# Seven Strassen column pairs, each interleaved with an ordinary one, and all their sums on VectorE

## Chip, cores and metric

The kernel runs on one core of one Trainium2 chip. The metric is the device time of one execution in microseconds (us). Three runs of the kernel before took 884.0 us in the median (883.87 to 885.13). Engines are called by the profile's short names: PE (matrix products), PEld (its weight loads), DVE (VectorE), ACT (ScalarE), POOL (GpSimd) and SP, whose queue issues the DMAs.

## The reference

One layer for 512 tokens of width 1024: an mLSTM and an S5 mixer, and behind them a gated feed-forward net with a hidden width of 2816. The change lies in the feed-forward net alone, in its first product:

```python
def _conv_glu_ffn(h, w_ffn_up, w_ffn_conv, b_ffn_conv, w_ffn_down):
    val, gate = jnp.split(h @ w_ffn_up, 2, axis=-1)
    gate = jax.nn.gelu(_causal_dwconv(gate, w_ffn_conv, b_ffn_conv))
    return (gate * val) @ w_ffn_down
...
        h = _standardize(x) * (1.0 + sc2) + sh2
        f = _conv_glu_ffn(h, w_ffn_up[l], w_ffn_conv[l], b_ffn_conv[l], w_ffn_down[l])
        x = _layer_norm(ALPHA * x + (1.0 + g2) * f, ln2_gain[l], ln2_bias[l])
```

`_causal_dwconv` has three taps here. Everything is computed in float32.

## The kernel before

The hidden width is cut into 22 tiles of 128 (`j` = 0 to 21). For each `j` the kernel makes a gate tile and a value tile, each 128 x 512 (channels by tokens), with the 1024 inputs in eight pieces of 128 (`k`). A float32 factor is written as the sum of two fp32r numbers, `hi` and `lo`, and a product is three matmuls: hi·hi, hi·lo, lo·hi (`mm3`, lines 247 to 249). So an ordinary tile is 24 matmuls of 128 x 512, and an ordinary `j` is 48.

The splitting costs ACT and DVE work: ACT casts a weight tile to its high part (line 226), DVE subtracts to get the low part (line 215). `wsplit` does it for an ordinary tile (128 x 1024), from the buffers `w` (two) to `wh` and `wl` (three each).

Ten of the 22 `j` are made by Strassen's scheme in Winograd's form (`fast_pairs`). The gate and value weights of one `j` and the two halves of `k` give a 2 x 2 block matrix, the halves of `k` and of the tokens another. Seven half-size products, each 12 matmuls of 128 x 256 (`prod`, line 1264), stand for eight. Their weight operands are `a11`, `a12`, `a22` and four sums `r3`, `r2`, `r1`, `r4` (`fast_operands`); their `h` operands are quarters of `h2` and four combinations in the `hp` buffers, which `x_combos` makes once. Each weight operand is split by `half` (ACT on line 1227, DVE on line 215). Two sums of products, `d` and the upper half of `cv`, are made on DVE from PSUM, and the second must be read before the next product goes on in the same bank.

In `fast_pairs` two neighbouring `j` go through four parts together: `first` (a, c), `second` (b, a), `third` (b, d), `fourth` (b). The pairs begin at `FAST` = 5, 8, 11, 14, 17, and one ordinary `j` stands between two pairs. Both `a` and both `c` come from the four PSUM banks called `hd`. The same four banks hold the scratch of the gelu (`gate_half`, which calls `gelu2`, lines 566 to 570): ACT squares into the bank, DVE, ACT (tanh) and DVE follow, and the last DVE instruction, `hh<-hd,hh` on line 207, gives the bank back. The names `gtile` (called `acc` in the trace) and `vtile` (`s` in the trace, tag `s5`) are two banks each for gate and value products.

All eight small sums `gtt(...)` of `fast_operands` of a pair, and 16 of the 32 sums of `x_combos`, run on POOL (line 350, which is the helper `gtt`). `MODS` says after which `j` one slice of the last modulation vector (`g2`) is added up: each step is two DMAs of 128 x 512 into `hh` buffers and two DVE instructions into `s5h`. `NSP` = 19: the activations of `j` below 19 are written to DRAM (`spill`) and read again for the down product; those of 19 to 21 stay in SBUF. There are seven `hh` buffers.

The order of each engine's instructions is fixed when the program is built: a scheduler places each engine's work by its own reckoning of when inputs are there. Each engine then works strictly through its row and waits at an instruction until its inputs have come.

Of the kernel before, what the change touches and what calls it, by code (L numbers as in the profile page):

```python
# [162 lines left out]
def _build(ctx, tc, nc, h):  # L163
# [1103 lines left out]
    def fast_operands(j):  # L1267
# [7 lines left out]
        return a11, r3, r2, a12, r1, a22, r4

    def fast_pairs(js):
        src = [fast_operands(j) for j in js]
        a, c, b, d, cv = {}, {}, {}, {}, {}
        for j in js:  # L1280
            b[j], d[j] = gtile[j % 2], vtile[j % 2]

        def op(i, n):
            return half(src[i][n])

        def first(i, j):
            a[j], c[j] = bank("hd"), bank("hd")
            cv[j] = hh()
            prod(a[j], op(i, 0), xq(0, 0), True)
            A.copy(b[j][:, 0:256], a[j][:, 0:256])  # L1290
            prod(c[j], op(i, 1), xc(3), True)
            A.copy(cv[j][:, 0:256], c[j][:, 0:256])

        def second(i, j):
            prod(b[j], op(i, 2), xc(2))
            tt(d[j][:, 0:256], b[j][:, 0:256], cv[j][:, 0:256], ALU.add)
            prod(a[j], op(i, 3), xq(1, 0))

        def third(i, j):
            prod(b[j], op(i, 4), xc(1))  # L1300
            tt(cv[j][:, 256:512], b[j][:, 0:256], cv[j][:, 0:256], ALU.add)
            prod(d[j], op(i, 5), xc(4))

        def fourth(i, j):
            prod(b[j], op(i, 6), xq(1, 1))
# [88 lines left out]
```

## Time and profile before

| | |
|---|---|
| median of 3 runs | 884.0 us |
| the profiled execution: its time / its span | 885.54 / 883.8 us |
| PE busy | 826.0 us (93%), 4466 matmuls |
| DVE busy | 675.0 us (76%), 1240 instructions |
| ACT busy | 391.8 us (44%) |
| POOL busy | 173.7 us (20%) |
| mean granted PE clock | 0.987 of full speed |

The profiled execution took 1.54 us more than the median of the runs. Of its own time 1.7 us lie outside the span, which runs from the first to the last instruction. The first product of the feed-forward net fills the span from about 476 to 753 us, the down product from there to 876 us. In the timeline a row may merge several equal instructions; a start and a duration are given, and in brackets the engine's idle time before it and what ended it. Busy times of DVE overlap a little: an instruction may start before the record of the last one ends.

### The profile page before, as it was taken

Reading aid. Unit: us, or ns where it says so; the run is one execution under the profiler, and the core shown is the slowest. Engines: PE = TensorE matmul, PEld = TensorE weight load, DVE = VectorE, ACT = ScalarE, POOL = GpSimd, SP = SyncE. Lnnn points to the kernel's source line nnn. Section 1 sums busy time; section 2 is a strip of 40 time slices with the busy share of each in tenths; the row PEclk is TensorE's granted clock in tenths of the full one; section 3 lists DMA queues with packets and bytes.
Section 4 is the critical chain, followed back from the end, with each engine's and each line's share of the span. In section 5 each row is a group of like instructions: output and inputs, shape, how many; then the busy total and the mean of one; then the engine's idle time right before and its main releaser. Section 6 shows DMA issues by size and latency. Waiting matters only on the chain.

```text
span 883.8 us, 12383 instructions
## 1 busy us (share of the span) xinstructions
PE 826.0 (93%) x4466; PEld 682.2 (77%) x4466; DVE 675.0 (76%) x1240; ACT 391.8 (44%) x665; POOL 173.7 (20%) x289
## 2 busy tenths in 40 slices
PE   3999999999999999999999889989789998999996
PEld 1777878787777788888888868978778886788885
DVE  5557988789689755579888898797978767999144
ACT  4454565546456432323344555544454444545000
POOL 2771221122121000000003662342222000000000
PEclk9999999999999999999999989999999999999998
DMA  9832121322212445487552055423443243667011
GB/s 342 295 100 83 59 94 57 80 59 67 82 37 89 126 130 180 141 286 239 186 193 75 1 202 167 130 98 110 141 131 120 84 153 121 212 216 239 25 47 48
DMA packets 50893, 115.98 MB, mean 131 GB/s; under 512 B 13968, under 2 KB 14864, under 8 KB 50832
## 3 DMA queue, kind: packets, MB, share of 16 engines
q1 hardware_dynamic: 50832, 115.19, 39.6%
q8 instruction: 35, 0.57, 0.3%
q14 instruction: 26, 0.21, 0.1%
HBM read 105.99 MB, written 7.08 MB: 128 GB/s over the span
## 4 chain that ended last, share of the span: by engine, by line
PE 64%; DVE 21%; ACT 6%; issue 4%; DMA 3%; SPq 2%; POOL 1%; DVEq 0%; ACTq 0%; POOLq 0%
PE acc L247 8%; PE acc L249 8%; PE acc L248 8%; PE hd L247 6%; DVE hh L207 6%; PE hd L248 6%; PE hd L249 6%; PE acc L1264 4%; PE hd L1264 3%; PE s L247 2%; PE s L248 2%; PE s L249 2%; PE s L1264 2%; SPq L197 2%; DVE wl L215 1%
## 5 line engine op out<-in xcount | busy, mean ns | idle before, releaser
L226 ACT CAST wh<-w 128x1024 fp32r<-128x1024 f32 (+2 forms) x83 | 82.4, 995 | 109.7 <-PE acc L248 64.8
L215 DVE TENSOR_TENSOR wl<-w,wh 128x1024 fp32r<-128x1024 f32 (+2 forms) x83 | 99.0, 1195 | 21.9 <-ACT wh L226 19.1
L247 PE MATMUL acc<-hp,wh 128*128 128x512 f32 x256 | 103.3, 404 | 0.4 <-ACT hx L790 0.4
L248 PE MATMUL acc<-hp,wh 128*128 128x512 f32 x256 | 101.9, 398 | 0.0
L249 PE MATMUL acc<-hp,wl 128*128 128x512 f32 x256 | 101.8, 398 | 0.0
L1029 POOL TENSOR_SCALAR mov<-mov 128x1 f32<-128x1 f32 x6 | 4.1, 688 | 344.5 <-ACT acc L1028 172.6
L247 PEld LDWEIGHTS acc<-hp,wh 128*128 128x128 f32 x256 | 48.2, 189 | 14.7 <-issue 3.7
L249 PEld LDWEIGHTS acc<-hp,wl 128*128 128x128 f32 x256 | 48.2, 188 | 11.2 <-issue 0.4
L248 PEld LDWEIGHTS acc<-hp,wh 128*128 128x128 f32 x256 | 48.2, 188 | 10.8 <-issue 0.4
L207 DVE SCALAR_TENSOR_TENSOR s5h<-hh,k,s5h 128x512 f32<-128x512 f32 x56 | 44.9, 842 | 5.9 <-DMA hh<-in_wa 5.9
L207 DVE SCALAR_TENSOR_TENSOR hh<-hd,hh 128x512 f32<-128x512 f32 (+3 forms) x40 | 24.4, 609 | 21.0 <-ACT hd L569 12.3
L350 POOL TENSOR_TENSOR hx<-gab,gab 128x512 f32<-128x512 f32 x10 | 15.1, 1508 | 99.6 <-DMA gab<-in_wup 90.1
L350 POOL TENSOR_TENSOR hx<-gab,hx 128x512 f32<-128x512 f32 x20 | 32.6, 1632 | 4.8 <-DVE hb L215 3.4
L248 PE MATMUL hd<-s5b,wh 128*128 128x512 f32 (+1 forms) x88 | 32.2, 367 | 0.5 <-DVE s5b L215 0.5
L247 PE MATMUL hd<-s5b,wh 128*128 128x512 f32 (+1 forms) x88 | 31.8, 367 | 0.7 <-ACT s5b L1180 0.5
L249 PE MATMUL hd<-s5b,wl 128*128 128x512 f32 (+1 forms) x88 | 31.9, 363 | 0.0
L567 ACT ACTIVATE hd<-hh 128x512 f32<-128x512 f32 x22 | 13.2, 601 | 40.9 <-DVE hh L207 40.8
L248 PE MATMUL acc<-hx,wh 128*128 128x512 f32 x74 | 29.2, 394 | 0.0
L247 PE MATMUL acc<-hx,wh 128*128 128x512 f32 x74 | 29.1, 394 | 0.0
L249 PE MATMUL acc<-hx,wl 128*128 128x512 f32 x74 | 29.1, 393 | 0.0
L1264 PE MATMUL hd<-hp,hb 128*128 128x256 f32 x120 | 17.7, 300 | 11.5 <-DVE hh L207 11.5
L212 DVE TENSOR_TENSOR hh<-w,hh 128x512 f32<-128x512 f32 x42 | 27.3, 685 | 1.1 <-DMA w<-in_wfd 1.1
(626 smaller groups left out, 2392.9 us busy)
## 6 DMA issues: line engine op xcount, KB each, us to landing
hh<-in_wa SPq DMA_DIRECT2D x64, 256.0 KB, 4.2
w<-in_win SPq DMA_DIRECT2D x30, 512.0 KB, 3.3
w<-in_wup SPq DMA_DIRECT2D x24, 512.0 KB, 3.8
w<-in_wfd SPq DMA_DIRECT2D x22, 512.0 KB, 4.1
gab<-in_wup SPq DMA_DIRECT2D x20, 512.0 KB, 3.6
hb<-in_wa SPq DMA_DIRECT2D x16, 512.0 KB, 7.3
spill<-hh SPq DMA_DIRECT2D x19, 256.0 KB, 2.0
hh<-spill SPq DMA_DIRECT2D x19, 256.0 KB, 3.4
```

Of the source, the lines that this page charges most:

```text
L197: return nc.sync.dma_start(o, i)
L207: V.scalar_tensor_tensor(o, i0, s, i1, op0=op0, op1=op1)
L212: V.tensor_tensor(o, a, b, op=op)
L215: V.tensor_tensor(o, a, b, op=ALU.subtract)
L226: A.copy(hi, x)
L247: T.matmul(o, lhsT=wh, rhs=xh, start=first, stop=False)
L248: T.matmul(o, lhsT=wh, rhs=xl, start=False, stop=False)
L249: T.matmul(o, lhsT=wl, rhs=xh, start=False, stop=last)
L350: GP.tensor_tensor(o, a, b, op=op)
L567: A.activation(a, x, AF.Square, scale=GELU_S)
L1029: GP.tensor_scalar(v[:, 2:3], v[:, 0:1], v[:, 1:2], EPS * D, op0=ALU.add, op1=ALU.add)
L1264: T.matmul(o[:, 0:256], lhsT=w[:, p, sl], rhs=x[k][y], start=first and k + i == 0, stop=k == 3 and i == 2, skip_group_check=True)
```

## The change

`fast_pairs` goes. In its place `fast_and_plain(j)` makes `j` by the seven products and `j + 1` in the ordinary way, with the ordinary one's two tiles in halves of 12 matmuls (`part`) between the seven products. `FAST` is now 6, 8, 10, 12, 14, 16, 18, so seven `j` are made by Strassen's scheme, not ten, and 13 by ordinary products behind the two of the start, not ten. The sums of `fast_operands` and of `x_combos` are all on DVE (`tt`), none on POOL. `x_combos` is called before `j` = 3, not 4. `MODS` is 5, 6, 8, 10, 12, 14, 16, 18. `NSP` is 20: the activation of `j` = 19 goes through DRAM too. All split operands now lie in the six `hb` buffers.

```diff
-FAST = (5, 8, 11, 14, 17)
-XJ = 4
-MODS = (7, 10, 10, 13, 13, 16, 16, 19)
-NSP = 19
+FAST = (6, 8, 10, 12, 14, 16, 18)
+XJ = 3
+MODS = (5, 6, 8, 10, 12, 14, 16, 18)
+NSP = 20
...
-    optag = iter((("hb",) * 6 + ("wh", "wl") * 3 + ("hb",) * 2) * NF)
+    optag = iter(("hb",) * (8 * NF))
...
-            gtt(xk[k][:, lo_], f32(h2[k][0])[:, lo_], f32(h2[k][1])[:, lo_], ALU.add)
+            tt(xk[k][:, lo_], f32(h2[k][0])[:, lo_], f32(h2[k][1])[:, lo_], ALU.add)
...
-        gtt(r3, a11, a21, ALU.subtract)
...
+        tt(r3, a11, a21, ALU.subtract)
...
-    def fast_pairs(js):
...
-        for part in (first, second, third, fourth):
-            for i, j in enumerate(js):
-                part(i, j)
-        for j in js:
-            gg = gate_half(j, (a[j], b[j]))
-            val_half(j, gg, (d[j], cv[j][:, 256:512]))
+    def fast_and_plain(j):
+        src = fast_operands(j)
+        b, d = gtile[j % 2], vtile[j % 2]
+        g2_, v2_ = gtile[1 - j % 2], vtile[1 - j % 2]
+        a, c = bank("hd"), bank("hd")
+        cv = hh()
...
+        prod(a, half(src[0]), xq(0, 0), True)
+        A.copy(b[:, 0:256], a[:, 0:256])
+        prod(c, half(src[1]), xc(3), True)
+        A.copy(cv[:, 0:256], c[:, 0:256])
+        wg_ = wsplit(h["wup"][2 * j + 3])
+        part(g2_, wg_, 0)
+        prod(b, half(src[2]), xc(2))
+        tt(d[:, 0:256], b[:, 0:256], cv[:, 0:256], ALU.add)
+        prod(a, half(src[3]), xq(1, 0))
+        part(g2_, wg_, 1)
+        prod(b, half(src[4]), xc(1))
+        tt(cv[:, 256:512], b[:, 0:256], cv[:, 0:256], ALU.add)
+        prod(d, half(src[5]), xc(4))
+        gg2 = gate_half(j + 1, (g2_,))
+        wv_ = wsplit(h["wup"][2 * j + 2])
+        part(v2_, wv_, 0)
+        prod(b, half(src[6]), xq(1, 1))
+        gg = gate_half(j, (a, b))
+        val_half(j, gg, (d, cv[:, 256:512]))
+        part(v2_, wv_, 1)
+        val_half(j + 1, gg2, (v2_,))
```

On PE, the start of the second pair (`j` = 8 and 9) before, one row for each run of matmuls with the same operands; `hd_5843` and `hd_5878` are the two `a`, `hd_5844` and `hd_5879` the two `c`:

```order
L1264 MATMUL hd_5843<-s5b_4721,hb_5846 128x256 x3
L1264 MATMUL hd_5843<-s5b_4722,hb_5846 128x256 x3
L1264 MATMUL hd_5843<-s5b_4723,hb_5846 128x256 x3
L1264 MATMUL hd_5843<-s5b_4724,hb_5846 128x256 x3
L1264 MATMUL hd_5844<-hp_5343,hb_5862 128x256 x6
L1264 MATMUL hd_5844<-hp_5344,hb_5862 128x256 x6
L1264 MATMUL hd_5878<-s5b_4721,hb_5881 128x256 x3
L1264 MATMUL hd_5878<-s5b_4722,hb_5881 128x256 x3
L1264 MATMUL hd_5878<-s5b_4723,hb_5881 128x256 x3
L1264 MATMUL hd_5878<-s5b_4724,hb_5881 128x256 x3
L1264 MATMUL hd_5879<-hp_5343,hb_5897 128x256 x6
L1264 MATMUL hd_5879<-hp_5344,hb_5897 128x256 x6
```

The same place in the changed kernel, at `j` = 10 with the ordinary 11 (`acc_4896` is the gate tile of 11, `hd_5987` and `hd_5988` are `a` and `c` of 10):

```order
L249 MATMUL acc_4896<-s5b_4721,wl_6025 128x512
L247 MATMUL acc_4896<-s5b_4722,wh_6024 128x512
L1264 MATMUL hd_5987<-s5b_4721,hb_5990 128x256 x3
L1264 MATMUL hd_5987<-s5b_4722,hb_5990 128x256 x3
L1264 MATMUL hd_5987<-s5b_4723,hb_5990 128x256 x3
L1264 MATMUL hd_5987<-s5b_4724,hb_5990 128x256 x3
L1264 MATMUL hd_5988<-hp_5271,hb_6006 128x256 x6
L1264 MATMUL hd_5988<-hp_5272,hb_6006 128x256 x6
L248 MATMUL acc_4896<-s5b_4722,wh_6024 128x512
L249 MATMUL acc_4896<-s5b_4722,wl_6025 128x512
```

Before, a pair opens all four `hd` banks at once, 48 matmuls in a row. Now a stage opens two, and matmuls of the ordinary tile stand ahead of them and behind.

On DVE, the rows before the same pair: the gelu of the ordinary `j` = 7 (`hd_5774` is its scratch bank), its value product, and what follows; `hb_6037` and `hb_6052` are low parts of the last operands of the pair 8 and 9, `hb_6210` is the first of the next:

```order
L207 SCALAR_TENSOR_TENSOR hh_5769<-acc_4896,k_63,hh_5769 128x510
L215 TENSOR_TENSOR wh_6006<-hx_5837,wh_6006 128x512
L207 SCALAR_TENSOR_TENSOR hh_5769<-acc_4896,k_63,hh_5769 128x511
L215 TENSOR_TENSOR wl_6022<-gab_5833,wl_6022 128x512
L207 SCALAR_TENSOR_TENSOR hd_5774<-hd_5774,hh_5769 128x512
L207 SCALAR_TENSOR_TENSOR hh_5773<-hd_5774,hh_5769 128x512
L212 TENSOR_TENSOR hh_5773<-s_1059_4898,hh_5773 128x512
L215 TENSOR_TENSOR hb_6037<-hx_5826,hb_6037 128x512
L215 TENSOR_TENSOR hb_6052<-hx_5838,hb_6052 128x512
L201 TENSOR_SCALAR s5h_5811<-hh_5813,k_92 128x512
```

On DVE in the changed kernel, from the sum `d` of `j` = 8 on; `hb_6006` to `hb_6056` are low parts for `j` = 10, `hx_6199` and `hx_6200` sums for `j` = 12, `wl_6127` is the low part of an ordinary tile of 11, `hh_5771` the `cv` of 8, `hh_5896` the gate of 9:

```order
L212 TENSOR_TENSOR s_1058_4897<-acc_4895,hh_5771 128x256
L207 SCALAR_TENSOR_TENSOR s5h_5532<-hh_5754,k_92,s5h_5532 128x512
L215 TENSOR_TENSOR hb_6006<-hx_5979,hb_6006 128x512
L212 TENSOR_TENSOR hx_6199<-hx_6198,gab_6193 128x512
L215 TENSOR_TENSOR hb_6040<-hx_5980,hb_6040 128x512
L212 TENSOR_TENSOR hx_6200<-gab_6193,hx_6198 128x512
L215 TENSOR_TENSOR wl_6127<-w_6124,wh_6126 128x1024
L212 TENSOR_TENSOR hh_5771<-acc_4895,hh_5771 128x256
L207 SCALAR_TENSOR_TENSOR hh_5896<-acc_4896,k_63,hh_5896 128x510
L215 TENSOR_TENSOR hb_6056<-gab_5975,hb_6056 128x512
```

The sums, which stood on POOL, now stand between the splits; the splits on DVE are for the stage after the one that PE is in, the sums for the one after that.

On DVE, the rows before the first ordinary weight of the product (`wl_5198`, for `j` = 2), in the kernel before; `hp_...` are the low parts of the combinations of `h`, `gab_...` holds the combinations themselves:

```order
L212 TENSOR_TENSOR gab_5065<-gab_5065 128x256
L215 TENSOR_TENSOR hp_5344<-gab_5039,hp_5344 128x512
L215 TENSOR_TENSOR hp_5341<-gab_5052,hp_5341 128x512
L215 TENSOR_TENSOR hp_5342<-gab_5065,hp_5342 128x512
L215 TENSOR_TENSOR hp_5339<-gab_5026,hp_5339 128x512
L215 TENSOR_TENSOR hp_5340<-gab_5039,hp_5340 128x512
L215 TENSOR_TENSOR hp_5345<-gab_5052,hp_5345 128x512
L215 TENSOR_TENSOR hp_5346<-gab_5065,hp_5346 128x512
L215 TENSOR_TENSOR wl_5198<-w_5195,wh_5197 128x1024
```

And in the changed kernel:

```order
L212 TENSOR_TENSOR gab_5052<-gab_5052,gab_5026 128x256 x2
L212 TENSOR_TENSOR gab_5052<-gab_5052 128x256 x2
L212 TENSOR_TENSOR gab_5065<-gab_5065,gab_5039 128x256 x2
L212 TENSOR_TENSOR gab_5065<-gab_5065 128x256 x2
L215 TENSOR_TENSOR hp_5271<-gab_5026,hp_5271 128x512
L215 TENSOR_TENSOR hp_5272<-gab_5039,hp_5272 128x512
L215 TENSOR_TENSOR hp_5269<-gab_5052,hp_5269 128x512
L207 SCALAR_TENSOR_TENSOR hh_5171<-hd_4905,k_63,hh_5171 128x510
L215 TENSOR_TENSOR wl_5198<-w_5195,wh_5197 128x1024
```

Sixteen more sums stand ahead of the weight, five of the eight splits have gone behind it, and one instruction of the first gate has come in front of it.

## Rows read from the trace of the kernel before

**Rows 1.** The page: busy time of each engine with its share of the span, and the share of each engine in the chain of waits that ended last.

```profile
PE 826.0 (93%) x4466; PEld 682.2 (77%) x4466; DVE 675.0 (76%) x1240; ACT 391.8 (44%) x665; POOL 173.7 (20%) x289
...
PE 64%; DVE 21%; ACT 6%; issue 4%; DMA 3%; SPq 2%; POOL 1%; DVEq 0%; ACTq 0%; POOLq 0%
```

**Rows 2.** Stretches of the five Strassen pairs, from their first matmul to the next ordinary one: bounds and length in us, busy us (and instructions) of PE, PEld, DVE, ACT and POOL, granted PE clock, DMA share, GB/s.

```profile
547.35:567.05 19.70, 19.70 (x169) 19.70 (x168) 14.55 (x20) 11.10 (x21) 9.23 (x6) 1.00 0.38 121
578.45:604.54 26.09, 21.88 (x170) 21.47 (x169) 21.86 (x29) 13.27 (x25) 6.83 (x5) 0.93 0.37 123
615.93:643.68 27.75, 21.99 (x170) 21.35 (x169) 23.93 (x31) 13.39 (x25) 7.53 (x5) 0.94 0.41 135
655.05:681.98 26.93, 21.90 (x169) 21.48 (x168) 22.59 (x31) 12.85 (x24) 7.83 (x5) 0.94 0.41 138
693.36:713.94 20.58, 20.14 (x170) 19.93 (x169) 13.79 (x21) 9.31 (x16) 0.00 (x0) 1.00 0.42 131
```

**Rows 3.** The same view for two of the four ordinary `j` between the pairs (7 and 16).

```profile
567.05:578.45 11.40, 11.40 (x51) 8.96 (x50) 9.96 (x12) 4.69 (x10) 5.65 (x4) 1.00 0.32 111
...
681.98:693.36 11.38, 11.38 (x50) 8.95 (x49) 9.13 (x16) 6.37 (x12) 0.00 (x0) 1.00 0.06 23
```

**Rows 4.** What PE waited for between 547 and 730 us: total us, times, longest.

```profile
PE hd L1264 <- DVE hh L207: 12.5, 6, 3.8
PE acc L1264 <- DVE s L212: 3.0, 2, 1.5
```

**Rows 5.** PE's timeline: two undisturbed products of the first pair, and the start of the second pair with the wait in it.

```profile
561.39 1.58 PE L1264 MATMUL acc<-hp,wh 128*128 128x256 f32 x12
562.80 1.57 PE L1264 MATMUL s<-hp,wl 128*128 128x256 f32 x12
...
587.34 1.99 PE L1264 MATMUL hd<-hp,hb 128*128 128x256 f32 x12 [3.80 <-DVE hh L207]
589.12 2.76 PE L1264 MATMUL acc<-hp,hb 128*128 128x256 f32 x12
```

**Rows 6.** DVE's timeline ahead of that wait.

```profile
574.67 1.78 DVE L215 TENSOR_TENSOR wh<-hx,wh 128x512 fp32r<-128x512 f32 x1
576.37 1.78 DVE L207 SCALAR_TENSOR_TENSOR hh<-hh,k,hh 128x511 f32<-128x511 f32 x1
...
583.18 0.68 DVE L215 TENSOR_TENSOR wh<-hx,wh 128x512 fp32r<-128x512 f32 x1
583.78 0.74 DVE L207 SCALAR_TENSOR_TENSOR hh<-acc,k,hh 128x511 f32<-128x511 f32 x1
```

**Rows 7.** POOL's timeline in the same stretch.

```profile
575.98 1.63 POOL L350 TENSOR_TENSOR hx<-hx,gab 128x512 f32<-128x512 f32 x1
```

**Rows 8.** Groups of DVE instructions by line and shape between 682 and 753 us, where POOL does nothing: busy us, mean ns of one, and the idle time before them with what ended it.

```profile
L215 DVE TENSOR_TENSOR wl<-w,wh 128x1024 fp32r<-128x1024 f32 x6 | 7.3, 1224 | 2.4 <-ACT wh L226 1.3 <-PE s L1264 1.0
L207 DVE SCALAR_TENSOR_TENSOR hh<-hd,hh 128x512 f32<-128x512 f32 x10 | 6.9, 691 | 4.6 <-ACT hd L569 4.5
L207 DVE SCALAR_TENSOR_TENSOR hd<-hd,hh 128x512 f32<-128x512 f32 x8 | 5.6, 698 | 3.2 <-ACT hd L567 2.9
L207 DVE SCALAR_TENSOR_TENSOR s5h<-hh,k,s5h 128x512 f32<-128x512 f32 x6 | 4.3, 746 | 2.3 <-DMA hh<-in_wa 2.3
L207 DVE SCALAR_TENSOR_TENSOR hh<-hh,k,hh 128x510 f32<-128x510 f32 x4 | 3.0, 749 | 1.4 <-ACT hh L1204 1.4
...
L212 DVE TENSOR_TENSOR hh<-s,hh 128x512 f32<-128x512 f32 x4 | 2.8, 692 | 0.8 <-PE s L249 0.5
...
L215 DVE TENSOR_TENSOR hb<-hx,hb 128x512 fp32r<-128x512 f32 x3 | 2.0, 685 | 1.0 <-ACT hb L1227 1.0
L212 DVE TENSOR_TENSOR hh<-s,hh 128x256 f32<-128x256 f32 x4 | 1.7, 424 | 0.1
```

**Rows 9.** What DVE waited for between 547 and 730 us: total us, times, longest.

```profile
DVE hh L207 <- ACT hd L569: 10.4, 16, 0.6
...
DVE hd L207 <- ACT hd L567: 5.1, 7, 0.7
DVE s5h L207 <- DMA hh<-in_wa: 3.0, 3, 2.3
```

**Rows 10.** DMA issues between 547 and 753 us: count, KB each, median us from issue to landing.

```profile
hh<-in_wa SPq DMA_DIRECT2D x16, 256.0 KB, 4.0
```

**Rows 11.** PE's timeline where the products of the first two `j`, made in two token halves, have ended and the ordinary `j` = 2 begins.

```profile
509.29 0.50 PE L247 MATMUL acc<-s5b,wh 128*128 128x512 f32 x1 [2.69 <-ACT wh L226]
...
511.90 0.79 PE L249 MATMUL acc<-s5b,wl 128*128 128x512 f32 x1 [1.88 <-DVE wl L215]
...
519.36 0.39 PE L247 MATMUL s<-s5b,wh 128*128 128x512 f32 x1
```

**Rows 12.** DVE's timeline ahead of it.

```profile
492.83 1.81 DVE L215 TENSOR_TENSOR s5b<-gab,s5b 128x256 fp32r<-128x256 f32 x2
...
500.94 0.94 DVE L212 TENSOR_TENSOR gab<-gab,gab 128x256 f32<-128x256 f32 x1 [2.71 <-POOL gab L350]
...
503.81 0.75 DVE L212 TENSOR_TENSOR gab<-gab,gab 128x256 f32<-128x256 f32 x2
...
510.64 1.21 DVE L215 TENSOR_TENSOR wl<-w,wh 128x1024 fp32r<-128x1024 f32 x1
```

**Rows 13.** The down product as one stretch, in the view of rows 2.

```profile
753.00:876.00 123.00, 122.89 (x552) 100.28 (x552) 79.99 (x136) 37.02 (x68) 2.95 (x6) 1.00 0.43 137
```

More of the change, by code (lines that the diff above doesn't have):

```diff
@@ L1240, in x_combos @@
         for k in range(KD):
-            gtt(xk[k][:, lo_], f32(h2[k][0])[:, lo_], f32(h2[k][1])[:, lo_], ALU.add)
+            tt(xk[k][:, lo_], f32(h2[k][0])[:, lo_], f32(h2[k][1])[:, lo_], ALU.add)
         for k in range(4):
-            gtt(xk[k][:, lo_], xk[k][:, hi_], xk[k][:, lo_], ALU.subtract)
-            gtt(xk[k][:, hi_], xk[k + 4][:, hi_], xk[k][:, hi_], ALU.subtract)
+            tt(xk[k][:, lo_], xk[k][:, hi_], xk[k][:, lo_], ALU.subtract)
+            tt(xk[k][:, hi_], xk[k + 4][:, hi_], xk[k][:, hi_], ALU.subtract)
         for k in range(4):
@@ L1270, in fast_operands @@
         r3, r2, r1, r4 = (hx() for _ in range(4))
-        gtt(r3, a11, a21, ALU.subtract)
-        gtt(r2, a22, r3, ALU.subtract)
-        gtt(r1, r2, a11, ALU.add)
-        gtt(r4, a12, r2, ALU.subtract)
+        tt(r3, a11, a21, ALU.subtract)
+        tt(r2, a22, r3, ALU.subtract)
+        tt(r1, r2, a11, ALU.add)
+        tt(r4, a12, r2, ALU.subtract)
         return a11, r3, r2, a12, r1, a22, r4
-    def fast_pairs(js):
-        src = [fast_operands(j) for j in js]
-        a, c, b, d, cv = {}, {}, {}, {}, {}
-        for j in js:
[L1281 to L1305, printed above, removed]
-        for part in (first, second, third, fourth):
-            for i, j in enumerate(js):
-                part(i, j)
-        for j in js:
-            gg = gate_half(j, (a[j], b[j]))
-            val_half(j, gg, (d[j], cv[j][:, 256:512]))
@@ new lines, in fast_and_plain, with part @@
+    def fast_and_plain(j):
[4 more added lines that the diff above has]
+        cv = hh()
+        def part(o, w, n):
+            for k in range(4 * n, 4 * n + 4):
+                sl = slice(k * P, (k + 1) * P)
+                mm3(o, w[0][:, sl], w[1][:, sl], h2[k][0], h2[k][1], k == 0, k == KD - 1)
+        prod(a, half(src[0]), xq(0, 0), True)
[19 more added lines that the diff above has]
+        val_half(j + 1, gg2, (v2_,))
@@ L1334, in _build @@
         if j in FAST:
-            fast_pairs((j, j + 1))
+            fast_and_plain(j)
         elif j - 1 not in FAST:
```

## The prediction

> **What bounds the kernel now.** I read the page first, then the stretches of the feed-forward net by windows, PE's waits in them, and last the timelines of DVE and POOL ahead of those waits. PE is busy 93% of the span and is most of the chain of waits [rows 1], so a change is worth what it takes from PE's work or from PE's waits. The down product has no wait to speak of: 122.89 us busy in 123 [rows 13]. The first product has: the five Strassen pairs are the same work on PE, yet they take 19.70, 26.09, 27.75, 26.93 and 20.58 us [rows 2]. The first runs without a wait. Over it the others lose 6.39 + 8.05 + 7.23 + 0.88 = 22.55 us.
>
> The loss has two layers. PE waits 12.5 us for a bank `hd` that DVE's last gelu instruction has to give back, and 3.0 us for the sum `d` [rows 4]. And after the 3.80 us wait of the second pair twelve matmuls that take 1.41 us from start to start in the first pair take about 2.5 [rows 5]: the granted clock of these stretches is 0.93 or 0.94 and not 1.00 [rows 2], so some of it ran at the lower of the two levels. That is 15.5 us of waits and some 7 us of slow clock and smaller gaps.
>
> Why is DVE late with the gelu? While POOL makes a sum, a DVE instruction on SBUF takes 1.78 us, and without it 0.74 or 0.68 [rows 6]: POOL's sum of 575.98 us lies across one of them [rows 7]. Four such instructions ahead of a pair cost DVE some 4 us, about the 3.80 that PE waits. The fifth pair, with no POOL at work in its stretch, loses only 0.88 [rows 2]. Waits and POOL go together.
>
> **The change part by part.**
>
> *More ordinary work: +4.6 us.* A Strassen `j` takes 19.70 / 2 = 9.85 us of PE [rows 2], an ordinary one 11.38 [rows 3]. Ten Strassen `j` become seven, so three times 1.53 is added, all of it on PE.
>
> *The pairs' waits: -22.55 us, and what is late next.* By the order a stage opens two `hd` banks and not four, and the gelu scratch of the two gates lies in the other two. The bank of the next `c` is free once ACT has copied the last `a` out, which it can do right behind the seventh product; between that and `c` PE has 12 + 4 ordinary matmuls and 12 of `a`, 2.8 + 0.9 + 1.4 = 5.1 us. The sum `d` has to be made between the third and the fifth product; there stand now 12 matmuls of 256 and 12 of 512 columns, 4.2 us, and before only two products, 2.8. So neither wait has to come back if DVE keeps its place.
>
> Does it? A stage of `j` and `j + 1` has 9.85 + 11.38 = 21.23 us of PE. DVE has 28 instructions in it: seven low parts of 0.685 (4.80), two of 1.224 (2.45), four sums, same shape as a low part, 0.685 (2.74), two gates of 2 x 0.749 + 0.698 + 0.691 (5.77), the value products 0.692 + 2 x 0.424 (1.54), `d` and `cv` 2 x 0.424 (0.85), two steps of the modulation 2 x 0.746 (1.49): 19.6 us [rows 8]. An instruction starts 0.60 us after one that lasted 0.68 [rows 6], 0.08 sooner than the record says, so the row really costs 19.6 - 28 x 0.08 = 17.4 us. Its own waits for ACT, in each gate one of 0.7 for the square and one of 0.65 for the tanh [rows 9], would make 20.1 if nothing stood in them; in the changed order low parts stand in most. 17.4 to 20.1 is under 21.23. The splits run almost a whole stage ahead of PE (six `hb` buffers), so a late one is not felt at once. I take 1 us for all seven stages together, for first and last stages that are not yet in step; the bounds are -2 (the 0.2 us with which an ordinary tile begins may vanish between the products) and +24 (rival 1).
>
> The four sums cost DVE 4 x 0.60 = 2.4 us of a stage. On POOL each took 1.6 us and cost DVE 1.0 besides, 4 x 1.04 = 4.2 us, so DVE gains by taking them over. [...]
>
> *The start of the ordinary products: -5 us.* PE stands idle 2.69 and 1.88 us there, and the gate tile of `j` = 2, which 11.38 / 2 = 5.7 us would do, lasts from 506.60 (509.29 - 2.69) to 519.36, 12.8 us [rows 11]: 7.1 us lost, slow clock included. DVE ends the awaited low part at 511.85 [rows 12]. Against that the new row ahead of it has: no wait for POOL (-2.71); low parts of 256 columns that take 0.4 and not 0.9 or 0.65 us (about -3, from six or seven such); five splits gone behind it (5 x 0.60, -3.0); sixteen sums more (16 x 0.34 by 503.81 us, +5.4); one instruction of the gate (+0.66). Sum -2.7, so it ends near 509.2. PE has four matmuls (0.9 us) to do before it needs it, so some 1.7 us are lost and not 7.1. Bounds: 0 (ACT's casts come no sooner) and -7.1. I take -5.
>
> *Moved without a price.* The steps of `MODS` are the same eight; a stage now has one, two DMAs of 256 KB with 4.0 us to landing [rows 10], and DVE's longest wait for one was 2.3 [rows 9]. In the new SP row they stand behind the load of an ordinary weight, whose buffer DVE frees some 4 to 5 us ahead of the step. Without that cover the step waits up to 2.3 us in every stage (rival 1). The activation of `j` = 19 goes out and comes back, 256 KB each way, with a cast and a low part (0.7 us on DVE) in the down product, where DVE is busy 80 us of 123 [rows 13]. That of the end of the first product (last modulation step, `g2`, first down weights) stays in the same order; I leave it at 0, +-1.
>
> *Sum.* 885.5 (the profiled execution's own time) + 4.6 - 22.55 - 5 + 1 = 863.6. That execution was 1.5 over the median of the runs shown: 862.
>
> **The rivals.**
>
> 1. *DVE becomes the bound of a stage.* For it: 19.6 us of records and 2.7 of waits are above 21.23, and the DMA wait of 2.3 may come on top. 20.1 + 2.3 = 22.4 us would be 1.2 over PE's 21.23, seven times 8 us, less the 1 us I already count: 869. With no overlap of instructions 24.6, 3.4 over, 24 us: 885. Against it: the starts in rows 6. Nearest to the lower end: 870.
>
> 2. *PE waits for a bank or a sum in every stage, longer than before: slower.* The mechanism is one late gate: if ACT copies `a` out only after it has waited for DVE's gelu of `j + 1`, which stands ahead of it in ACT's row, `c` of the next stage waits, as the pairs did for their banks. Price: the mean of pairs two to four, 7.2 us, in each of seven stages, 50.5 in place of the 22.55 that the sum takes away: 862 - 1 + 50.5 = 911. It decides from 3.2 us per stage on (22 / 7). For it: the same chain of DVE and ACT instructions is the one that PE waited for [rows 4]. Against: 5.1 us of other matmuls stand between.
>
> 3. *The start gives nothing*, since ACT and not DVE is last there or the sixteen sums take longer: 867.
>
> **How the numbers follow.** The forecast, 858 to 866, has 0.67; the start without gain (867) 0.12; DVE-bound (870, with a tail to 885) 0.14; slower (911) 0.07. Faster by over 0.2% (1.8 us, about what a measurement of this kernel tells from no change) are all but the last and a sliver of the third: 0.91; within 0.2%: 0.02; slower: 0.07. The range that leaves out two in ten is 857 to 872: below it lies a start with no loss at all and stages without the small gaps, above it the upper half of rival 1 and rival 2.
>
> **What would show it.** Right: seven stages of about 21.2 us on PE, granted clock 1.00 in them, no `hd L1264 <- DVE` in PE's waits, POOL idle after about 498 us, DVE instructions of 512 columns at 0.7 us throughout and never at 1.78, and the first `wl` of `j` = 2 done near 509. Wrong: stages longer than 21.5 with DVE busy over 20 us in each (rival 1), a clock under 1.00 in the stages (rival 2), or waits of DVE for `in_wa` in each stage. If DVE still shows 1.78 us with POOL idle, the reading of the cause was wrong, and the gain would be what the bank order alone gives.

## The result and the profile after

The changed kernel takes 860.72 us (median of four runs, 859.15 to 861.58), the kernel before beside it 883.93 us (883.25 to 885.13). The ratio is 0.9734 with an interval of 0.9716 to 0.9752, so 23.2 us are gone. The forecast was 862.0 with a range of 857 to 872.

The page of the profile after, the busy time of each engine and the chain that ended last by engine, answers to [rows 1]:

```profile
PE 818.5 (95%) x4358; PEld 672.8 (78%) x4358; DVE 651.4 (76%) x1260; ACT 382.5 (45%) x638; POOL 95.5 (11%) x233
PE 74%; DVE 13%; DMA 4%; ACT 4%; issue 2%; SPq 2%; POOL 0%; DVEq 0%; ACTq 0%; POOLq 0%
```

The seven stages as windows, from the first matmul of the Strassen `j` to that of the next one; the columns are those of [rows 2], which holds the five pairs of before:

```profile
549.49:571.57 22.08, 22.08 (x138) 19.75 (x137) 15.63 (x24) 11.15 (x20) 0.00 (x0) 1.00 0.33 111
571.57:592.70 21.13, 21.13 (x134) 19.00 (x132) 17.84 (x29) 11.06 (x21) 0.00 (x0) 1.00 0.44 150
592.70:613.83 21.13, 21.13 (x133) 19.00 (x132) 17.84 (x29) 11.06 (x21) 0.00 (x0) 1.00 0.46 149
...
677.23:698.36 21.13, 21.13 (x133) 19.01 (x132) 12.33 (x20) 7.33 (x14) 0.00 (x0) 1.00 0.29 100
```

PE is busy in every microsecond of every stage, the granted clock is 1.00, and POOL does nothing. The first window is 0.95 longer only because of where the stages are cut: from the second on, four matmuls of the next ordinary tile stand ahead of the Strassen product in PE's row, so the first window has four more (138 for 134). DVE is busy 17.84 us of 21.13.

PE's waits from 500 to 740 us (line waited for: total, times, longest), to be read beside [rows 4]. No wait for `hd` at L1264 and none for the sum is left:

```profile
PE acc L247 <- ACT hx L226: 2.0, 1, 2.0
PE acc L247 <- ACT wh L226: 1.6, 2, 0.8
PE s L247 <- ACT wh L226: 0.7, 2, 0.5
PE acc L249 <- DVE wl L215: 0.7, 1, 0.7
PE s L249 <- DVE wl L215: 0.5, 1, 0.5
```

PE's timeline of after at four places: the first matmul of the second token half (the first two `j` are made in two token halves), the start of ordinary `j` = 2 [rows 11], two waits of `j` = 21, and the first matmul of the down product:

```profile
489.83 0.39 PE L247 MATMUL hd<-s5b,wh 128*128 128x256 f32 x1 [0.55 <-ACT s5b L1180]
...
504.28 0.50 PE L247 MATMUL acc<-s5b,wh 128*128 128x512 f32 x1 [0.82 <-ACT wh L226]
...
505.23 0.50 PE L247 MATMUL s<-s5b,wh 128*128 128x512 f32 x1 [0.22 <-ACT wh L226]
...
717.71 0.50 PE L247 MATMUL s<-s5b,wh 128*128 128x512 f32 x1 [0.47 <-ACT wh L226]
...
718.97 0.50 PE L249 MATMUL s<-s5b,wl 128*128 128x512 f32 x1 [0.54 <-DVE wl L215]
...
726.30 0.50 PE L247 MATMUL acc<-wh,hx 128*128 128x512 f32 x1 [1.95 <-ACT hx L226]
```

The first and last of these in the trace of before:

```profile
492.27 0.50 PE L247 MATMUL hd<-s5b,wh 128*128 128x256 f32 x2 [0.55 <-ACT s5b L1180]
...
752.95 0.50 PE L247 MATMUL acc<-wh,hx 128*128 128x512 f32 x1 [1.95 <-ACT hx L226]
```

These two marks bound nearly all that the change touches but the down product. Ahead of the first lies the first token half, beside which the first of the sixteen sums are made: from its first matmul (479.34 before, 477.32 after) to the mark it is 12.93 us before and 12.51 after. The mark itself moves by up to 4.6 us from one profiled execution to another (489.29 to 493.87 in the 14 traces of this case), so spans are a poor measure of a few microseconds. The text below uses the length between the marks and calls it the first product, though the first token half is left out. It was 752.95 - 492.27 = 260.68 us and is 726.30 - 489.83 = 236.47: 24.2 less. (The profiled spans differ by 26.4, 2.4 of it ahead of the first mark: the profiled execution of before, 885.54 us, is longer than all four runs of before in this comparison, that of after is the fastest of its four.)

The 24.2 by place, with the rows of before and the marks above. An ordinary `j` is taken at 11.38 us and a Strassen one at 9.85, as the prediction did.

| Part of the first product | before | after | difference | forecast |
|---|---|---|---|---|
| three `j` made ordinary | | | +4.6 | +4.6 |
| from the first mark to the first Strassen product, less its ordinary `j` (3, then 4) | 547.35 - 492.27 - 34.14 = 20.94 | 549.49 - 489.83 - 45.52 = 14.14 | -6.8 | -5 |
| pairs, then stages, over their plain work (144.0, then 148.6) | 166.59 - 144.02 = 22.57 | 147.94 - 148.61 = -0.67 | -23.2 | -22.55 + 1 |
| from there to the down product, less its ordinary `j` (3, then 2) | 39.01 - 34.14 = 4.87 | 28.87 - 22.76 = 6.11 | +1.2 | 0, +-1 |

The stages end at 697.43, where the four matmuls of `j` = 20 begin that stand ahead of 698.36.

### The profile page after: what moved, and what is told of

Same layout as the page of the kernel before. It is cut to its first block, busy times and chain, and to the rows that moved or that the text cites. A ratio compares the mean times of both kernels' runs of the same rounds, so it can differ in the third digit from the quotient of the medians.

```text
span 857.4 us, 12051 instructions
## 1 busy us (share of the span) xinstructions
PE 818.5 (95%) x4358; PEld 672.8 (78%) x4358; DVE 651.4 (76%) x1260; ACT 382.5 (45%) x638; POOL 95.5 (11%) x233
## 4 chain that ended last, share of the span: by engine, by line
PE 74%; DVE 13%; DMA 4%; ACT 4%; issue 2%; SPq 2%; POOL 0%; DVEq 0%; ACTq 0%; POOLq 0%
PE acc L247 10%; PE acc L249 10%; PE acc L248 10%; PE hd L247 6%; PE hd L248 6%; PE hd L249 6%; PE s L247 4%; PE s L249 4%; PE s L248 4%; PE acc L1264 3%; PE hd L1264 3%; DVE hh L207 3%; SPq L197 2%; DVE s5h L212 1%; DVE wl L215 1%
## 5 line engine op out<-in xcount | busy, mean ns | idle before, releaser
L226 ACT CAST wh<-w 128x1024 fp32r<-128x1024 f32 (+2 forms) x89 | 88.7, 999 | 126.8 <-PE acc L248 89.1
L215 DVE TENSOR_TENSOR wl<-w,wh 128x1024 fp32r<-128x1024 f32 (+2 forms) x89 | 103.4, 1165 | 34.5 <-ACT wh L226 33.7
L207 DVE SCALAR_TENSOR_TENSOR s5h<-hh,k,s5h 128x512 f32<-128x512 f32 x56 | 39.7, 746 | 8.3 <-DMA hh<-in_wa 8.2
L207 DVE SCALAR_TENSOR_TENSOR hh<-hd,hh 128x512 f32<-128x512 f32 (+3 forms) x40 | 24.2, 607 | 15.7 <-POOL hh L859 8.4
L248 PE MATMUL acc<-hx,wh 128*128 128x512 f32 x77 | 30.4, 395 | 0.0
L247 PE MATMUL acc<-hx,wh 128*128 128x512 f32 x77 | 30.3, 394 | 0.0
L1227 ACT CAST hb<-hx 128x512 fp32r<-128x512 f32 x28 | 17.4, 621 | 26.0 <-PE acc L1264 15.4
L226 ACT CAST hb<-hh 128x512 fp32r<-128x512 f32 (+3 forms) x37 | 20.3, 550 | 17.2 <-DVE hh L207 11.1
L215 DVE TENSOR_TENSOR hb<-hh,hb 128x512 fp32r<-128x512 f32 (+3 forms) x37 | 22.1, 599 | 1.6 <-ACT hb L226 1.3
L1264 PEld LDWEIGHTS acc<-hp,hb 128*128 128x128 f32 x168 | 22.0, 188 | 1.3
```

Source lines behind the costliest of these rows:

```text
L207: V.scalar_tensor_tensor(o, i0, s, i1, op0=op0, op1=op1)
L215: V.tensor_tensor(o, a, b, op=ALU.subtract)
L226: A.copy(hi, x)
L247: T.matmul(o, lhsT=wh, rhs=xh, start=first, stop=False)
L248: T.matmul(o, lhsT=wh, rhs=xl, start=False, stop=False)
L1227: A.copy(o[:, 0], src)
```

## The experiments

Medians and ratios to the kernel before on the same chip; the last column is the first product in the profiled execution.

| Kernel | us (lowest to highest) | ratio, 95% interval | first product |
|---|---|---|---|
| before | 883.93 (883.25 to 885.13) | 1 | 260.7 |
| after | 860.72 (859.15 to 861.58) | 0.9734 (0.9716 to 0.9752) | 236.5 |
| before, sums on DVE | 864.65 (864.36 to 865.54) | 0.9788 (0.9765 to 0.9810) | 239.2 |
| after, all sums on POOL | 867.68 (865.32 to 869.06) | 0.9811 (0.9785 to 0.9838) | 243.4 |
| after, the operand sums on POOL | 862.51 (862.14 to 863.01) | 0.9764 (0.9737 to 0.9790) | 236.8 |
| after, the sixteen sums on POOL | 867.36 (866.94 to 868.64) | 0.9819 (0.9796 to 0.9842) | 243.0 |
| after, seven products in a row | 860.80 (858.42 to 863.12) | 0.9742 (0.9713 to 0.9771) | 235.0 |
| the same, operand sums on POOL | 864.27 (862.90 to 867.04) | 0.9763 (0.9736 to 0.9790) | 239.6 |
| after, unused sums on POOL | 868.44 (865.55 to 874.45) | 0.9815 (0.9771 to 0.9859) | 248.1 |
| after, unused memsets on POOL | 861.23 (860.83 to 863.17) | 0.9731 (0.9704 to 0.9758) | 236.9 |
| after, unused products by a constant on POOL | 860.79 (860.39 to 862.34) | 0.9730 (0.9714 to 0.9745) | 237.3 |
| after, an eighth stage in front | 861.46 (860.75 to 865.51) | 0.9737 (0.9706 to 0.9767) | 237.7 |
| after, eight stages at odd `j` | 866.64 (865.58 to 869.55) | 0.9803 (0.9782 to 0.9825) | 242.6 |
| after, 19 activations in DRAM | 861.25 (859.78 to 863.71) | 0.9734 (0.9715 to 0.9754) | 237.2 |

### One half alone: the sums on DVE, the pairs as they were

```diff
-            gtt(xk[k][:, lo_], f32(h2[k][0])[:, lo_], f32(h2[k][1])[:, lo_], ALU.add)
+            tt(xk[k][:, lo_], f32(h2[k][0])[:, lo_], f32(h2[k][1])[:, lo_], ALU.add)
...
-        gtt(r3, a11, a21, ALU.subtract)
+        tt(r3, a11, a21, ALU.subtract)
...
```

> The kernel before with its pairs as they were (two products in a row, four pairs of banks), but every sum that POOL made from the loaded matrices (four per pair, and the sixteen sums of the activations' part ahead) on DVE. Theory A, the waits for the bank and for the sum come from DVE's long instructions while POOL reads SBUF: DVE's 512-column sums stay at 0.68 to 0.74 us throughout, each of the five pairs takes about as long as the first and the last of before (some 20 us), the gap at the start of ordinary product 2 shrinks, and the time falls by some 20 us, to 861 to 866. Theory B, the waits come from the order of a pair itself (two quarters that reuse a bank without other work between them): most of the loss stays, and only the start gains, about 878 to 880.

864.65 us, 19 less than before: POOL's part is the larger one, as theory A says. But the pairs are not free of loss. PE's waits from 530 to 690 us, and two stretches from the start of a pair to that of the next (pair and one ordinary `j`, 19.70 + 11.38 = 31.08 without loss):

```profile
PE hd L1264 <- DVE hh L207: 4.2, 4, 1.3
PE s L247 <- DVE hh L212: 1.6, 3, 0.6
```

```profile
542.20:574.01 31.81, 31.27 (x218) 28.80 (x216) 28.80 (x48) 17.75 (x33) 0.00 (x0) 1.00 0.51 165
574.01:607.35 33.34, 31.46 (x218) 28.80 (x216) 28.39 (x48) 18.08 (x34) 0.00 (x0) 1.00 0.39 135
```

The same wait for the `hd` bank stands there, a third as long as in [rows 4], with no POOL in sight. By the sum of the table above the five pairs lose 693.93 - 542.20 - 144.02 = 7.7 us in place of 22.6 (693.93 is where the ordinary `j` behind the last pair begins). At the start 14.4 is left of 20.9, nearly all of what the whole change gives there. The granted clock is 1.00: a bank that came 1.3 late cost its own wait and little more (PE is busy 31.27 and 31.46 us in the two stretches, for 31.08 of plain work), where the waits of up to 3.8 in [rows 4, 5] went with slow matmuls besides: behind that of 3.80 us the granted clock is 0.50 from 588.70 to 591.70 and 1.00 again from 592.00.

The windows show one thing more, DVE's load. In the kernel before, from the start of the second pair to that of the third, DVE is busy longer than the 31.08 us that PE's plain work takes:

```profile
578.45:615.93 37.48, 33.27 (x217) 30.42 (x216) 31.82 (x40) 17.82 (x34) 11.89 (x9) 0.95 0.36 120
```

With the sums on DVE it is 28.80 and 28.39 of 31.08, or 91 to 93%. In the kernel after it is 17.84 of 21.13, or 84%: a stage with one Strassen `j` leaves DVE more room than a pair.

### The other half alone: the new order, all sums on POOL

```diff
-            tt(xk[k][:, lo_], f32(h2[k][0])[:, lo_], f32(h2[k][1])[:, lo_], ALU.add)
+            gtt(xk[k][:, lo_], f32(h2[k][0])[:, lo_], f32(h2[k][1])[:, lo_], ALU.add)
...
-        tt(r3, a11, a21, ALU.subtract)
+        gtt(r3, a11, a21, ALU.subtract)
...
```

> The other half of the change by itself: the kernel after with its seven interleaved stages, but all twenty kinds of sums on POOL as before (four per stage and the sixteen ahead). Theory A, the two halves are independent: POOL costs nothing that shows in the stages (the run with the operand sums on POOL) and some 6.5 us at the start (the run with the sixteen sums there), 867 to 870, so the order alone gives most of the gain in the pairs. Theory B, DVE comes late out of the start and, slowed by POOL in every stage, doesn't catch up: the first stages wait, 872 or more.

867.68 us: theory A. PE's timeline at the start of ordinary `j` = 2 has the waits of before [rows 11] back to 0.01 us:

```profile
506.31 0.51 PE L247 MATMUL acc<-s5b,wh 128*128 128x512 f32 x1 [2.69 <-ACT wh L226]
...
508.92 0.80 PE L249 MATMUL acc<-s5b,wl 128*128 128x512 f32 x1 [1.87 <-DVE wl L215]
```

From the first mark to the first stage it takes 555.64 - 489.29 - 45.52 = 20.8 us besides the ordinary `j`, 6.7 more than in the kernel after, and the stages still begin every 21.13 us (619.98, 641.11, 662.25, 683.38 are four of these starts), with four sums on POOL (6.2 us) in each of the second to fifth. So the order, with all that changes beside it but the engine of the sums, takes away the whole loss of the pairs, and nothing at the start.

### The two groups of sums apart

```diff
-        tt(r3, a11, a21, ALU.subtract)
+        gtt(r3, a11, a21, ALU.subtract)
...
```

> The kernel after, with the four sums of each stage's operands on POOL again; the interleaving stays. Theory A, DVE slowed by POOL is the whole cause and cover does not help: DVE's sums go to 1.78 us beside POOL, the waits for the bank come back, and the time goes to 875 or more. Theory B, the ordinary product in quarters gives DVE enough slack to hide the slow sums: at most 1 us per stage, 861 to 867.

862.51 us; the interval overlaps that of after. Theory B. A stage of it in the view of windows, and DVE's instructions by form from 545 to 690 us (count, busy, mean ns of one, idle time before):

```profile
573.16:594.30 21.14, 21.14 (x134) 19.00 (x133) 16.89 (x25) 11.08 (x21) 6.22 (x4) 1.00 0.43 149
```

```profile
L215 DVE TENSOR_TENSOR hb<-gab,hb 128x512 fp32r<-128x512 f32 x18 | 15.5, 859 | 5.4 <-ACT hb L1227 5.4
...
L212 DVE TENSOR_TENSOR hh<-hh,hh 128x256 f32<-128x256 f32 x6 | 5.5, 922 | 0.0
```

In the kernel after, the same two forms take 686 and 414 ns. DVE is slowed by POOL here too, yet it is busy 16.89 us with four instructions fewer, against 17.84 with all of them, and PE has no gap. Taking four sums (2.7 us of records) off DVE puts 1.8 us back on it, so moving them to DVE costs the row about 1 us of busy time; the prediction had it gain 1.8.

```diff
-            tt(xk[k][:, lo_], f32(h2[k][0])[:, lo_], f32(h2[k][1])[:, lo_], ALU.add)
+            gtt(xk[k][:, lo_], f32(h2[k][0])[:, lo_], f32(h2[k][1])[:, lo_], ALU.add)
...
```

> The kernel after, with the sixteen sums of the activations' part ahead of the stages on POOL again. Theory A (the prediction's term for the start): the first low part of ordinary product 2 is late again by some 5 us, and the time is 864 to 867. Theory B, ACT's copies are what comes last there: no difference, 860 to 862.

867.36 us, 6.6 over after: theory A, a little above its range. The waits at `j` = 2 are 2.72 and 1.77 us. With the run before it this settles where POOL's sums hurt in the new kernel: at the start alone.

### Is the interleaving needed?

Seven products in a row, the ordinary pair of matrices behind them; sums on DVE:

```diff
         A.copy(cv[:, 0:256], c[:, 0:256])
-        wg_ = wsplit(h["wup"][2 * j + 3])
-        part(g2_, wg_, 0)
         prod(b, half(src[2]), xc(2))
...
         val_half(j, gg, (d, cv[:, 256:512]))
+        wg_ = wsplit(h["wup"][2 * j + 3])
+        part(g2_, wg_, 0)
+        part(g2_, wg_, 1)
...
```

> The kernel after with the seven products of a pair in a row again, and the ordinary pair behind them; the sums stay on DVE. Theory A, the cover is needed for the two sums between products that share a bank: two waits of 1 to 1.5 us in each of seven stages, some 14 to 21 us, 875 to 882. Theory B, DVE without POOL beside it is early enough without cover: 860 to 864.

860.80 us: theory B, and the cover that the prediction counted on is not needed. PE has no wait at all from 530 to 690 us, and a stage is as long as with quarters:

```profile
574.29:595.40 21.11, 21.11 (x133) 19.02 (x132) 17.95 (x29) 11.20 (x20) 0.00 (x0) 1.00 0.44 149
```

The first product is even 1.5 us shorter, 1.3 of it behind the last stage, where two of the four short waits at the end are absent; the medians do not show it.

The same order with the operand sums on POOL:

```diff
-        tt(r3, a11, a21, ALU.subtract)
+        gtt(r3, a11, a21, ALU.subtract)
...
```

> Seven products in a row, as in the run before of that order, and in addition each stage's four operand sums on POOL. Theory A, cover matters only while DVE is slow, and the quarters hid POOL's cost: now the bank wait and the sum wait are back, about 1 to 3 us per stage, 868 to 882. Theory B, one Strassen j per stage with two banks is what removes the waits, whatever engine makes the sums and wherever the ordinary products stand: 860 to 864.

864.27 us, between the theories. PE waits for the sum again, twice from 530 to 690 us, and a stage without such a wait takes 21.55:

```profile
PE acc L1264 <- DVE s L212: 1.5, 2, 0.9
```

```profile
572.09:593.64 21.55, 21.42 (x134) 19.10 (x133) 18.25 (x24) 11.09 (x20) 5.69 (x4) 1.00 0.42 147
```

The two waits, 0.53 and 0.94, are in the first stage (21.90) and the fifth (22.51). The first six stages take 130.17 us here and 126.64 in the run before with the sums on DVE. With quarters and POOL's operand sums no stage loses anything. So the quarters hide 3.5 us in all, 0.4 to 1.4 in each of five stages, and only with a slow DVE. The larger part of the pairs' 22.6 us goes with something else in the new stages: one Strassen `j` and not two stands between ordinary ones, with two `hd` banks and not four, with other buffers for the splits (`optag`), with one step of `MODS` per stage and not two ahead of a pair, and with DVE at 84% of PE's time and not at 91% or more. Which of these it is was not tried apart.

### What on POOL slows DVE?

Three kernels give POOL unused work in each stage of the kernel after; nothing waits for it but the buffer of one loaded matrix pair. First sums, which have two SBUF inputs:

```diff
+        gtt(scr, a11, a21, ALU.subtract)
+        for _ in range(5):
+            gtt(scr, scr, scr, ALU.subtract)
         tt(r3, a11, a21, ALU.subtract)
```

> The kernel after, with six sums of 128x512 that nobody uses added on POOL in each stage; they read and write SBUF, nothing waits for them but the buffers of the loaded matrices (the first reads two). Theory A, contention: while they run (about 10 us of a stage) DVE's instructions with two SBUF inputs go from 0.69 to 1.7 us or so, those with a PSUM input or with one input don't; DVE loses about 6 us per stage, has more than the 21.1 us of PE, and the time goes to 877 to 895. Theory B, it was not POOL's reads but the dependence of the splits on POOL's late sums: 860 to 862.

868.44 us: the direction of theory A, at less than its size. The profiled execution is the longest of its four, 874.45. POOL's six sums run from 601.60 to 609.87. DVE's timeline beside them and behind:

```profile
601.44 0.69 DVE L207 SCALAR_TENSOR_TENSOR hd<-hd,hh 128x512 f32<-128x512 f32 x1
602.04 1.40 DVE L212 TENSOR_TENSOR hx<-gab,gab 128x512 f32<-128x512 f32 x1
603.37 1.52 DVE L215 TENSOR_TENSOR hb<-hx,hb 128x512 fp32r<-128x512 f32 x1
604.81 0.68 DVE L207 SCALAR_TENSOR_TENSOR hh<-hd,hh 128x512 f32<-128x512 f32 x1
605.41 0.92 DVE L215 TENSOR_TENSOR hb<-gab,hb 128x512 fp32r<-128x512 f32 x1
606.26 0.41 DVE L212 TENSOR_TENSOR hh<-s,hh 128x256 f32<-128x256 f32 x1
606.59 0.93 DVE L212 TENSOR_TENSOR hh<-hh,hh 128x256 f32<-128x256 f32 x1
607.44 1.52 DVE L212 TENSOR_TENSOR hx<-gab,hx 128x512 f32<-128x512 f32 x1
608.89 1.52 DVE L207 SCALAR_TENSOR_TENSOR s5h<-hh,k,s5h 128x512 f32<-128x512 f32 x1
...
611.33 0.68 DVE L215 TENSOR_TENSOR hb<-hx,hb 128x512 fp32r<-128x512 f32 x1
```

Read the inputs in the names: `hd` and `s` are PSUM banks, the rest SBUF. With a PSUM input an instruction takes 0.69, 0.68 and 0.41 us beside POOL, with two SBUF inputs 0.92 to 1.52 (0.93 at 256 columns); once POOL is done, the form of 1.52 takes 0.68. POOL's 7.87 us put DVE at 21.66 us busy in the stage from 621.71 to 644.59, 3.8 more than in the kernel after and only 1.2 short of the whole stage; PE waits 1.4 to 1.5 us for the sum in three stages, which take 22.8 to 22.9. The size was off since six sums take 7.9 us and not 10, and only six of DVE's nine instructions beside them are of the kind that is slowed.

Then memsets, which only write:

```diff
+        gtt(scr[:, 0:1], a11[:, 0:1], a21[:, 0:1], ALU.subtract)
+        for _ in range(20):
+            GP.memset(scr, 0.0)
         tt(r3, a11, a21, ALU.subtract)
```

> The kernel after, with twenty memsets of 128x512 that nobody uses added on POOL in each stage (about 10 us of POOL, as in the run with unused sums): they write SBUF and read nothing. Theory A, POOL's reads are what slows DVE: DVE stays at 0.69 us, 860 to 862. Theory B, any access of POOL to SBUF slows DVE: as in the run with unused sums, 877 to 895.

861.23 us: theory A. POOL is at work longer than with the sums (11.64 us in a stage against 7.87), and DVE's stage stays at 17.85 us. POOL's timeline in one stage, then DVE's:

```profile
615.52 11.64 POOL L1276 MEMSET k<- 128x512 f32 x20
```

```profile
615.71 0.68 DVE L212 TENSOR_TENSOR hx<-gab,gab 128x512 f32<-128x512 f32 x1
616.33 0.69 DVE L215 TENSOR_TENSOR hb<-hx,hb 128x512 fp32r<-128x512 f32 x1
616.94 0.68 DVE L207 SCALAR_TENSOR_TENSOR hh<-hd,hh 128x512 f32<-128x512 f32 x1
617.54 0.68 DVE L215 TENSOR_TENSOR hb<-gab,hb 128x512 fp32r<-128x512 f32 x1
618.14 0.41 DVE L212 TENSOR_TENSOR hh<-s,hh 128x256 f32<-128x256 f32 x1
618.48 0.41 DVE L212 TENSOR_TENSOR hh<-hh,hh 128x256 f32<-128x256 f32 x1
618.81 0.68 DVE L212 TENSOR_TENSOR hx<-gab,hx 128x512 f32<-128x512 f32 x1
```

So for these instructions it is not POOL being busy or writing that costs: the five that take 1.40, 1.52, 0.92, 0.93 and 1.52 us beside POOL's sums take 0.68, 0.69, 0.68, 0.41 and 0.68 beside its memsets. The sums read SBUF, the memsets only write it. The two with a PSUM input take 0.68 and 0.41 beside either.

One form with a single SBUF input is slowed too, which theory A of the unused sums did not have: a product by a constant (`k`) that begins the sum of the modulation vector. Beside POOL's sums in the kernel before (two rows), with POOL idle in the kernel after, and beside memsets in this run:

```profile
589.48 1.18 DVE L201 TENSOR_SCALAR s5h<-hh,k 128x512 f32<-128x512 f32 x1 [0.27 <-DMA hh<-in_wa]
592.29 1.53 DVE L201 TENSOR_SCALAR s5h<-hh,k 128x512 f32<-128x512 f32 x1
...
553.25 0.48 DVE L201 TENSOR_SCALAR s5h<-hh,k 128x512 f32<-128x512 f32 x1
...
553.33 0.81 DVE L201 TENSOR_SCALAR s5h<-hh,k 128x512 f32<-128x512 f32 x1
```

There are two such instructions in the stages, so they weigh little here.

Last, products by a constant, which read one tile:

```diff
+        gts(scr, a11, -1.0)
+        for _ in range(6):
+            gts(scr, scr, -1.0)
         tt(r3, a11, a21, ALU.subtract)
```

> The kernel after, with seven unused products by a constant of 128x512 on POOL in each stage (about 8.6 us of POOL): each reads one SBUF tile and not two. Theory A, any POOL instruction that reads SBUF slows DVE's instructions with two SBUF inputs: they go well over 0.69 us, PE waits for the sum again, about 866 to 875, as with the unused sums. Theory B, only two reads at once on POOL do it: DVE stays at 0.69 us, 860 to 863.

860.79 us: the time of theory B, though DVE is not quite untouched. POOL's and DVE's timelines:

```profile
615.58 11.46 POOL L345 TENSOR_SCALAR k<-k 128x512 f32<-128x512 f32 x6
```

```profile
618.80 0.68 DVE L215 TENSOR_TENSOR hb<-hx,hb 128x512 fp32r<-128x512 f32 x1
...
624.00 1.10 DVE L215 TENSOR_TENSOR hb<-hx,hb 128x512 fp32r<-128x512 f32 x1
625.02 0.68 DVE L212 TENSOR_TENSOR hx<-hx,gab 128x512 f32<-128x512 f32 x1
```

Most DVE instructions take 0.68 us while POOL runs and a few 1.1; DVE is busy 18.88 us in a stage (594.93 to 616.07), 1.0 more than in the kernel after, and PE does not wait. POOL takes 1.9 us for one of its own instructions.

### An eighth stage

```diff
-FAST = (6, 8, 10, 12, 14, 16, 18)
+FAST = (4, 6, 8, 10, 12, 14, 16, 18)
```

> The kernel after with an eighth stage in front: the first Strassen j is 4 and not 6, so one ordinary j of 11.38 us becomes a Strassen j of 9.85. Theory A, stages are bound by PE alone: 1.5 us less, about 859. Theory B, DVE isn't ahead yet that early (the sixteen sums and the first sixteen splits of the loaded weights stand just before): the first stage waits, 861 or more.

861.46 us, first product 237.7 against 236.5: theory B. An ordinary tile just ahead of the first stage, at 529.43, waits 1.65 us until DVE's gelu (`hh`, L207) has read the bank `acc` of an earlier tile, a little more than the 1.5 that the eighth stage saves (the wait makes 0.1 of the 1.2 us, the rest stays open); low parts of the first stage stand between the gelu's steps in DVE's row.

```diff
-FAST = (6, 8, 10, 12, 14, 16, 18)
+FAST = (5, 7, 9, 11, 13, 15, 17, 19)
-MODS = (5, 6, 8, 10, 12, 14, 16, 18)
+MODS = (4, 5, 7, 9, 11, 13, 15, 17)
```

> The kernel after with eight stages at the odd numbers (5, 7, ... 19) in place of seven at the even ones (6, 8, ... 18): the first begins with ordinary j = 4 between it and the sixteen sums, one ordinary j fewer than in the kernel after. Theory A, stages are bound by PE alone and the early eighth stage of the former run failed for where it stood: 1.5 us less than after, about 859. Theory B, the eighth stage takes from the first product's end or its start what it gives: 861 to 863.

866.64 us, worse than either theory. From 561.74 to 667.41 its stages begin 21.13 us apart, the start has no new wait, and the loss is at the end of the first product, where only `j` = 21 stands behind the last stage. PE's timeline there:

```profile
711.55 0.50 PE L951 MATMUL hd<-hh,k 128*128 128x512 f32 x1 [2.66 <-ACT hh L226]
713.14 1.65 PE L951 MATMUL hd<-hh,k 128*128 128x512 f32 x3 [1.09 <-DVE hh L215]
717.98 0.79 PE L247 MATMUL acc<-s5b,wh 128*128 128x512 f32 x1 [3.19 <-ACT wh L226]
```

These 6.9 us are waits for the row that makes `g2` and for the split of the last tile's weights. Both wait for ACT and DVE, which still work off the last stage there (DVE itself waits 9.9 us for ACT's `hh`, L1204, from 690 to 740), and little ordinary work is left to hide that. The run moved the steps of `MODS` too; what each of the two does was not tried apart.

### Where the activations lie

```diff
-NSP = 20
+NSP = 19
```

> The kernel after with 19 activations kept in DRAM, as before, and not 20. The prediction priced the twentieth at nothing: 860 to 862. Rival, its cast, its low part and its two transfers cost the end of the first product or the down product something: 0.5 to 1.5 us less, 859 to 860.

861.25 us, ratio 0.9734 as after: no difference, as the prediction priced it.

## Why the prediction was right, point by point

- *More ordinary work, +4.6.* Right: a stage is 21.13 us of unbroken PE, 0.10 less than 9.85 + 11.38.
- *The pairs' waits, -22.55, and 1 us back.* The sum is right (-23.2), the loss was read from the windows of before and all of it went. What was wrong is what it was put down to. "Waits and POOL go together" is half of it, and [rows 2] spoke against the whole: the first pair has the most POOL work of the five, 9.23 us, and loses nothing; what it has little of is DVE work, 14.55 us where pairs two to four have 21.86 to 23.93. POOL's sums alone removed take 14.9 of the 22.6, and 7.7 stay with the old order and no POOL. The new order alone takes all 22.6, with POOL's sums in most stages. So the halves overlap, which is why the sum could be right for one reason too few. In [rows 6], 0.74 belongs to a gate instruction that reads a PSUM bank (`acc`); the SBUF form of it takes 0.749 without POOL [rows 8], so the size of the slowing stands.
- *What hides the waits.* The 5.1 us of ordinary matmuls ahead of `c` and the 4.2 us ahead of the fifth product were named as the cover. They are there, and with DVE alone they do nothing: without them no wait comes either. With the operand sums on POOL they hide 3.5 us in all stages together.
- *DVE's row, 17.4 to 20.1 us.* 17.84 measured, near the sum by starts, with a margin of 3.3 to PE. Rival 1 (DVE as the bound) did not come. The unused sums show it coming: with DVE at 21.66 us in a stage PE waits 1.4 to 1.5. In the second pair of before, with its ordinary `j`, DVE was already past it, 31.82 us of DVE for 31.08 of PE, which the prediction did not add up.
- *Four sums moved cost 2.4 and give back 4.2.* The second figure was too large for the new order: 1.8 us measured there. Part of POOL's work lies beside DVE instructions with a PSUM input, such as the one at 576.49 (0.68 us) in the run with the operand sums on POOL. In the old order it is about right: 31.82 us of DVE with eight sums on POOL, against 28.39 less 8 x 0.60 without sums, is an estimate of 1.0 per sum (both for the second pair and its ordinary `j`). So within a stage the move to DVE is a small loss of DVE time and not a gain, hidden in the margin: DVE is busy 17.84 us of 21.13.
- *The start, -5.* -6.8 measured, -6.7 by the run with all sums on POOL, near the bound of -7.1. Some 0.7 of it lies ahead of `j` = 2, where the term had nothing (from the mark to the start of the first wait, 14.33 us before and 13.63 after). The first low part of `j` = 2 ends on DVE at 505.70 (504.50 and 1.20 in its row), 15.9 us behind the first mark; 509.2 was forecast, which is 16.9 behind it in the execution of before. PE waits 0.82 and 0.22 there, both for ACT's casts and no longer for DVE, so the 1.7 us that the step left were too many. Rival 3 is out.
- *The end, 0 +-1.* +1.2, a little outside its bounds. Waits make 0.5 of it: those of 0.47 and 0.54 at 717.71 and 718.97 are new, and one for ACT's `wh` fell from 1.29 to 0.80. The other 0.7 is busy time of PE that no run explains.
- *The twentieth activation at nothing.* Right by the run with 19.
- *Rival 2 (a late gate in every stage)* did not come: ACT's copy of `a` is never what PE waits for in a stage.

The pairs gave 1.7 us more than forecast and the start 1.8, and the end took 1.2, so the misses cancel in part. In sum 885.5 + 4.6 - 23.2 - 6.8 + 1.2 = 861.3 for the first product's part, and 2.4 less ahead of the first mark in that execution give 858.9, against the 859.15 it took.
